# Plain columns in two halves of 336, up to five row blocks ahead of their norm, and the latent pairs interleaved

## The chip, the core and the metric

The kernel runs on one core of one Trainium2 chip. A time is the device time of one launch in microseconds (us), from the first to the last thing the core does for it; "before" is the median of three runs. Separate from these runs, one execution was recorded by the profiler, and all views of the profile and the trace come from that one. The engines are TensorE (PE in the rows; its weight loads are PEld), VectorE (DVE), ScalarE (ACT), GpSimd (POOL) and SyncE (SP), which issues most DMAs.

## The reference

One residual block over 1024 rows of 1024 columns, all in float32. Cut to what matters here:

```python
h = rmsnorm(x, mix_norm_g)
qa, ka, va, q_lat, kv_lat, k_r, g_a, g_b = split(h @ w_in)
#  512 128 128    384     256   32  1024 1024 columns
qa, ka = rope(qa), rope(ka)
o_a = sliding_window_attention(qa, ka, va, sinks)     # 8 heads, 2 kv heads, window 128
qb  = rmsnorm(q_lat, q_norm_g) @ w_uq                 # nope and rope part
kvb = rmsnorm(kv_lat, kv_norm_g) @ w_ukv              # k_nope and v
o_b = latent_attention(qb, kvb, rope(k_r))            # 8 heads, causal
y = sigmoid(g_a) * (o_a @ w_o_swa) + sigmoid(g_b) * (o_b @ w_o_mla)
x = x + y @ w_out
x = x + (silu(h2 @ w_gate) * (h2 @ w_up)) @ w_down    # h2 = rmsnorm(x, ffn_norm_g)
return rmsnorm(x, final_norm_g)
```

The change touches the first two lines and the first steps of the attention: the product of the normalised `x` with `w_in`, up to the point where the gate columns begin.

## The kernel before

**Products in halves.** A float32 operand is cut in a high part (ACT's cast, L160) and a low part (source minus high part, DVE, L163); this pair of instructions is `split` (L158). A product is then three passes on PE, high by high, high by low and low by high (`mm3`, L165 to L171: the three passes are lines L169, L170 and L171). Weights that carry the norm's gain are split with it (`split_g`, L229).

**Two kinds of columns of `w_in`.** The *plain* columns are multiplied as they stand: 512 columns of `qa` (`kvq`, L508; eight k-tiles of 128 rows by 512 columns, PSUM tile `kvq`) and 160 columns that hold `va` and `k_r` (`vk`, L483, tile `vk`), each once for each of the eight row blocks of 128 rows. The *latent* columns and `ka` (768 columns) go through a scheme with seven products instead of eight (`Seven`, L659): a pair j of column groups needs seven runs q = 1, 6, 2, 7, 5, 4, 3, each a product of one 512 by 128 weight (possibly a sum of quarters of the weight matrix) with one 512 by 512 quarter of `h`, or with a sum of quarters. A run is 12 passes of 512 columns. Three pairs, A, B and C, make 21 runs; `lat_head` (L985) is their order, and "A6" below is the run with j = A and q = 6. The gate columns use the same scheme behind it (`gates`).

**What a run needs.** The weight sums come from `mix` (L699; for the latent pairs six half-width instructions on POOL), after ACT scaled the weights by the gain (`scale_lt`, L916); a run's weight is split by `prep` (L713), tile `wl`. The sums of quarters of `h` come from `set_of_h` (L629), called once for each of four column groups c: it reads `h` back from memory (tiles `hr`, `ht`), subtracts, and splits the three results into `t1`, `t2`, `t3`. The run q = 6 multiplies by `t2`, 7 by `t3`, 5 by `t1`, 4 by `t4`; runs 1, 2 and 3 use the quarters of `h` themselves (`hh`, `hl`). The fourth sum is made on POOL at the end of `set_of_h` and split later (`t4_of_h`, L650).

**Where the rows of `h` come from.** For each row block b: `square(b)` (L460) takes the sum of squares on ACT and the factor `rn` on POOL; `spread(b)` (L468) lays the factor over the partitions by one small product; `normalize(b)` (L472) multiplies on DVE, and `to_quad(b)` (L475) splits the block into the quarter tiles. Blocks 0 to 4 (`RAW = 5`) are first split without their norm, so that `kvq` can start at once; `rope_q` (L499) multiplies their result by `rn` later, with the rotary tables, on DVE. `vk` of a block needs the normalised block. `vk_out` (L491) copies `v` and the rope key from PSUM. Block 0 is multiplied in plain float32 while its weights are split. `h_out` (L480) stores the normalised block for `set_of_h`, and `q_out` (L503) stores the rotated `qa` (`q_d`), which the sliding-window part loads back as `qn` and transposes on PE (`qT`).

**What follows a run.** `lat_done` (L962) takes the finished sum out of PSUM: for q-latent columns it scales, splits and stores it (`hi_lo_out`, L933, tile `cs`, store to `ct_d`) and squares it (`square_of`, L920); for the columns of `ka` it applies the rotation (`k_rope`, L947: four instructions on DVE, then a split into `ks`, stored to `ks_d`). The stores are issued by SP at the next `flush` (L942). Once all of `ks_d` is stored, four loads bring it back as `khd` for the first scores.

**The order.** Up to L1121 the order on PE, SP, ACT, DVE and POOL is written by hand: instructions stand in each engine's queue in the order of the calls. The plain part is L532 to L609 and L994 to L1044, with the calls `kvq`, `vk`, `normalize`, `to_quad` and so on; the latent runs are L1046 to L1120, one `lat_run(n)` (L989) each: it issues a run and then prepares weights up to the n-th. Tiles come from two pools with a fixed number of slots (U with 21, V with 17); a new tile waits until the last reader of its slot is done. [...]

Of the kernel before, what the change touches and what calls it, by code (L numbers as in the profile page):

```python
# [8 lines left out]
F32 = mybir.dt.float32  # L9
# [8 lines left out]
P = 128  # L18
# [24 lines left out]
VK = P + ROPE_B  # L43
# [44 lines left out]
def hybrid_block_kernel(  # L88
# [5 lines left out]
    w_x1: bass.AP,  # L94
    w_vk: bass.AP,
# [37 lines left out]
    psum_phase("psa", 4)  # L133
# [266 lines left out]
    w0 = st.raw[0] = U("wr", F32, (P, 2, 512))  # L400
# [3 lines left out]
    nc.scalar.dma_start(w0[:, 0], w_x1[:, 0])  # L404
# [3 lines left out]
    nc.sync.dma_start(w0[:, 1], w_x1[:, 1])  # L408
# [3 lines left out]
    st.load_to(3)  # L412
    load_xt(1)
    load_xt(2)
# [14 lines left out]
    def rope_nat(ps, heads, hw, cos, sin, outs, r=None):  # L429
        n = heads * 2 * hw  # L430
        t = U("rp")
        t1 = t[:, 0:n].rearrange("p (h t d) -> p h t d", t=2, d=hw)
        t2 = t[:, -n:].rearrange("p (h t d) -> p h t d", t=2, d=hw)
        cb = cos.unsqueeze(1).unsqueeze(1).to_broadcast([P, heads, 2, hw])
        sb = sin.unsqueeze(1).unsqueeze(1).to_broadcast([P, heads, 2, hw])
        for t_, b_ in ((t1, cb), (t2, sb)):
            if r is None:
                nc.vector.tensor_tensor(t_, ps, b_, op=ALU.mult)
            else:
                m_, p_ = (v.rearrange("p h t d -> p (h t) d") for v in (t_, ps))  # L440
                w_ = (cos if t_ is t1 else sin).unsqueeze(1).to_broadcast([P, heads * 2, hw])
                nc.vector.scalar_tensor_tensor(m_, p_, r, w_, op0=ALU.mult, op1=ALU.mult)
        for dst in outs:
            nc.vector.tensor_tensor(dst[:, :, 0], t1[:, :, 0], t2[:, :, 1], op=ALU.subtract)
            nc.vector.tensor_tensor(dst[:, :, 1], t1[:, :, 1], t2[:, :, 0], op=ALU.add)

    def halves(ap, hw):
        return ap.rearrange("p (h t d) -> p h t d", t=2, d=hw)

    def rope_of(ps, heads, b, r=None):  # L450
        qn = U("qn")
        rope_nat(halves(ps, 32), heads, 32, rope_a[:, 0, b], rope_a[:, 1, b], [halves(qn[:, 0:64 * heads], 32)], r)
        return qn

    wx1 = [halves_of((P, 2, 512), True) for _ in range(4)]
    kvq_ps, qns, sums, vk_ps = {}, {}, {}, {}
# [26 lines left out]
    def vk(b, mid=None):  # L483
        ps = vk_ps[b] = P1("vk", (P, VK))
        pairs = [(hT(k, blk(b)), tuple(w[:, k % 6] for w in wvk[k // 6])) for k in range(NK)]
        mm3(ps, pairs[:4], last=False)
        if mid is not None:
            mid()
        mm3(ps, pairs[4:], first=False)

    def vk_out(b):  # L491
        ps = vk_ps.pop(b)
        v_hi, v_lo = vv[b // 4][:, b % 4, :, 0:HD], vv[b // 4][:, b % 4, :, HD:P]
        v_ps = ps[:, 0:P].rearrange("p (g d) -> p g d", g=NG)
        nc.scalar.copy(v_hi, v_ps)
        nc.vector.tensor_tensor(v_lo, v_ps, v_hi.bitcast(F32), op=ALU.subtract)
        nc.scalar.copy(kr[:, 0, b], ps[:, P:VK])

    def rope_q(b):  # L499
        ps = kvq_ps.pop(b)  # L500
        qns[b] = rope_of(ps, 8, b, rn[:, b:b + 1] if b < RAW else None)
# [43 lines left out]
    for j in range(4):  # L545
        for k in (2 * j, 2 * j + 1):
            nc.tensor.matmul(ps, h0[:, k], raws[j][:, k % 2], start=k == 0, stop=k == NK - 1)
# [1637 lines left out]
```

## Time and profile before

| | us |
|---|---|
| three runs | 1386.88, 1385.52, 1385.92 |
| median | 1385.92 |
| profiled execution, its own time | 1383.58 |
| its span, first to last instruction | 1381.7 |
| PE busy in the span | 1322.0 |
| DVE, ACT, POOL busy | 931.2, 642.1, 586.7 |

The page lists busy time by engine, a bar of 40 slices of some 34.5 us each with the granted PE clock below it, and groups of instructions with the mean time of one and the idle time ahead of them. In rows of the trace the first number is the start in us from the span's start, the second the duration; x12 at a row's end means that several instructions alike stand in one row; a bracket at the end gives the idle time ahead of the instruction and what ended it. Rows name tiles without their numbers: `wl` is a split weight, `fa` and `fb` are the two kinds of PSUM tiles of the scheme with seven products.

### The profile page before, as it was taken

What the parts mean: (1) busy time and instruction counts of PE and PEld (TensorE: products, weight loads), DVE (VectorE), ACT (ScalarE), POOL (GpSimd) and SP (SyncE); (2) the same over time, 40 slices, a digit from 0 to 9 for tenths busy, and PEclk for the clock granted to TensorE, in tenths of its full rate; (3) what the DMA queues carried; (4) which work ended last, traced back from release to release, by engine and by line L of the source; (5) the groups of instructions that cost most, each with busy time, mean ns of one, the idle gap of its engine ahead of it and who ended that gap; (6) DMA issues with size and microseconds to landing.
All of it is one profiled execution on the core that took longest, in us unless ns stands there. A gap on an engine that the chain in (4) does not pass through costs nothing.

```text
span 1381.7 us, 18730 instructions
## 1 busy us (share of the span) xinstructions
PE 1322.0 (96%) x6376; PEld 1100.3 (80%) x6376; DVE 931.2 (67%) x1463; ACT 642.1 (46%) x1271; POOL 586.7 (42%) x627
## 2 busy tenths in 40 slices
PE   9964789999999999999999999999999999999997
PEld 6953578788878888988888888888888888888886
DVE  6754758778765877788787946656566565664763
ACT  6443246677534766774536422323223323644352
POOL 3063136556412554631232246778755552022421
PEclk9987889999999999999999999999999999999999
DMA  9721534553476847689742124555644324997504
GB/s 359 290 82 65 137 104 157 184 190 142 163 263 233 217 116 213 153 265 326 190 164 107 60 109 175 189 189 210 227 160 172 131 102 175 364 390 265 168 3 150
DMA packets 93456, 254.22 MB, mean 184 GB/s; under 512 B 10416, under 2 KB 16176, under 8 KB 91312
## 3 DMA queue, kind: packets, MB, share of 16 engines
q1 hardware_dynamic: 88496, 242.26, 50.2%
q0 software_dynamic: 3424, 8.39, 3.4%
q10 hardware_dynamic: 1440, 2.36, 0.5%
q8 instruction: 51, 0.84, 0.2%
q14 instruction: 45, 0.37, 0.1%
HBM read 166.60 MB, written 82.18 MB: 180 GB/s over the span
## 4 chain that ended last, share of the span: by engine, by line
PE 62%; issue 1%; POOL 1%; DVE 1%; ACT 0%; POOLq 0%; DVEq 0%
PE fa L171 6%; PE fa L169 6%; PE fa L170 6%; PE fd L170 5%; PE fd L171 5%; PE fd L169 5%; PE fb L170 4%; PE fb L171 4%; PE fb L169 4%; PE xo L171 2%; PE xo L170 2%; PE xo L169 2%; PE pTb L1348 1%; PE oB L171 1%; PE oB L170 1%
## 5 line engine op out<-in xcount | busy, mean ns | idle before, releaser
L163 DVE TENSOR_TENSOR wl<-wr,wl 128x512 fp32r<-128x512 f32 x165 | 156.0, 967 | 87.1 <-ACT wl L160 86.6
L163 DVE TENSOR_TENSOR lrv<-lr,lrv 128x1024 fp32r<-128x1024 f32 x77 | 105.5, 1402 | 47.8 <-ACT lrv L160 40.9
L160 ACT CAST lrv<-lr 128x1024 fp32r<-128x1024 f32 x77 | 80.1, 1052 | 87.2 <-PE fd L171 54.9
L169 PE MATMUL fd<-lrv 128*128 128x512 f32 x308 | 119.8, 389 | 0.0
L170 PE MATMUL fd<-lrv 128*128 128x512 f32 x308 | 119.8, 389 | 0.0
L171 PE MATMUL fd<-lrv 128*128 128x512 f32 x308 | 119.8, 389 | 0.0
L174 POOL TENSOR_TENSOR wr<-wr,sm 128x256 f32<-128x256 f32 (+1 forms) x44 | 50.7, 1165 | 137.9 <-DVE wl L163 122.4
L160 ACT CAST wl<-wr 128x512 fp32r<-128x512 f32 x165 | 95.6, 619 | 9.0 <-DVE t3l L174 2.8
L163 DVE TENSOR_TENSOR wl<-sm,wl 128x512 fp32r<-128x512 f32 x66 | 55.4, 860 | 42.7 <-ACT wl L160 41.3
L1333 POOL TENSOR_TENSOR denb<-denb,neg_one 128x1 f32<-128x1 f32 x64 | 41.5, 649 | 89.6 <-ACT p L1332 85.1
L169 PE MATMUL fa<-hh,wl 128*128 128x512 f32 x132 | 56.6, 429 | 21.6 <-ACT pu L761 18.2
L169 PEld LDWEIGHTS fd<-lrv 128*128 128x128 f32 x308 | 57.8, 188 | 12.1
L170 PEld LDWEIGHTS fd<-lrv 128*128 128x128 f32 x308 | 57.8, 188 | 12.0
L171 PEld LDWEIGHTS fd<-lrv 128*128 128x128 f32 x308 | 57.8, 188 | 12.0
L169 PE MATMUL fb<-t3h,wl 128*128 128x512 f32 x132 | 53.5, 405 | 11.5 <-ACT t4h L160 11.5
L1332 ACT ACTIVATE p<-scb,nmb 128x384 f32<-128x384 f32 (+3 forms) x64 | 47.7, 746 | 32.8 <-DVE nmb L1331 24.3
L1331 DVE CUSTOM_DVE_ANT_0 scb<-scb,mask,rlat 128x384 f32<-128x384 f32 (+3 forms) x64 | 52.1, 819 | 13.4 <-PE scb L1323 13.4
L171 PE MATMUL fa<-hh,wl 128*128 128x512 f32 x132 | 55.2, 418 | 0.2 <-DVE wl L163 0.2
L163 DVE TENSOR_TENSOR ptl<-pTb,pth 128x512 fp32r<-128x512 f32 (+2 forms) x96 | 49.9, 549 | 7.4 <-ACT pth L160 7.1
L170 PE MATMUL fa<-hl,wl 128*128 128x512 f32 x132 | 54.9, 416 | 0.0
L1706 ACT ACTIVATE act<-sm 128x512 f32<-128x512 f32 x11 | 7.0, 633 | 101.7 <-DVE sm L177 101.7
L170 PE MATMUL fb<-t3l,wl 128*128 128x512 f32 x132 | 53.1, 402 | 0.0
(371 smaller groups left out, 4163.8 us busy)
## 6 DMA issues: line engine op xcount, KB each, us to landing
lr<-la_d SPq DMA_DIRECT2D x77, 256.0 KB, 5.3
wr<-in_w_gate_dram SPq DMA_DIRECT2D x22, 512.0 KB, 4.2
wr<-in_w_up_dram SPq DMA_DIRECT2D x22, 512.0 KB, 4.9
la_d<-sd SPq DMA_DIRECT2D x22, 512.0 KB, 5.2
wd<-in_w_down_dram SPq DMA_DIRECT2D x22, 512.0 KB, 6.9
rb_d<-wd SPq DMA_DIRECT2D x22, 512.0 KB, 2.6
lr<-rb_d SPq DMA_DIRECT2D x44, 256.0 KB, 5.3
lr<-in_w_down_dram SPq DMA_DIRECT2D x33, 256.0 KB, 5.2
```

The costliest lines, as they stand in the source:

```text
L160: i = nc.scalar.copy(hi, src)
L163: (eng or nc.vector).tensor_tensor(lo, src, hi.bitcast(F32), op=ALU.subtract)
L169: nc.tensor.matmul(ps, ah, bh, start=first and i == 0, stop=False, skip_group_check=go_on)
L170: nc.tensor.matmul(ps, ah, bl, start=False, stop=False, skip_group_check=go_on)
L171: nc.tensor.matmul(ps, al, bh, start=False, stop=last and i == n - 1, skip_group_check=go_on)
L174: eng.tensor_tensor(out, a, b, op=ALU.subtract)
L1331: nc.vector.tensor_tensor_reduce(s_, s_, m_, rlat[:, n:n + 1], -NEG, op0=ALU.add, op1=ALU.min, accum_out=nm)
L1332: nc.scalar.activation(p_, s_, AF.Exp, scale=-1.0, bias=nm, accum_out=den)
L1333: nc.gpsimd.tensor_tensor(den, den, neg_one[:, 0:1], op=ALU.pow)
L1348: nc.tensor.transpose(pp[:, i], p[:, blk(k0 + i)], ident)
L1706: nc.scalar.activation(dst, src, AF.Silu)
```

## The change

**Plain columns.** `kvq` and `vk` give way to `nat(b, g)`: the plain columns are put together in two halves g of 336 columns (256 of `qa`, 64 of `va`, 16 of `k_r`), and both halves of a block are written to one PSUM tile `n` of two banks. The weights are loaded and split in units of three k-tiles. Blocks 0 to 4 are now multiplied without their norm in all their plain columns, and `row_out(b)` scales the copies of `v` and `k_r` and the rows of the rotary table by `rn` on ACT; the two rotary products on DVE then take the scaled table. Block 0 is in plain float32 in both halves (`nat0`).

**Rows and norms.** `norm_of(b)` is `normalize` and `to_quad` together. It stands up to five blocks behind the block's products, and blocks are normalised in the order 1, 5, 6, 2, 7, 0, 3, 4. The loads and squares follow that order.

**Sums of rows.** In `set_of_h` the subtraction that stood on POOL in two halves is one instruction on DVE, and the splits come in the order t2, t3, t1.

**Latent runs.** `lat_head` takes the first products of all three pairs ahead (A1, B1, C1, A2, B2, C2) and puts C's other runs between those of A and B. From the sixth run on a loop issues all of them and prepares two weights ahead of the run that it issues, that is, one ahead of the next. In this loop the loads of `qn` (`sw_q`) come ahead of the last `ks_d` stores and the `khd` loads, the load of `lg` and the store of the rope key come later, `gates.mix(0)` and the rotation of the rope key (`rope_kr`) go from DVE to POOL, and all gate scalings are on ACT.

```diff
-    for j in range(4):
-        plain(("x1", j), w_x1[:, 2 * j:2 * j + 2], (P, 2, 512), True, 2 * j)
-    plain(("vk", 0), w_vk[:, 0:6], (P, 6, VK), True, 0)
-    plain(("vk", 1), w_vk[:, 6:8], (P, 2, VK), False, 6)
+    for g in range(NG):
+        for u in range(3):
+            plain(("n", g, u), w_n[g, :, 3 * u:min(3 * u + 3, NK)], (P, min(3, NK - 3 * u), NW), True, 3 * u)
...
+    def scaled(b, dst, src):
+        if b < RAW:
+            nc.scalar.activation(dst, src, AF.Copy, scale=rn[:, b:b + 1])
+        else:
+            nc.scalar.copy(dst, src)
+    def row_out(b):
...
+        scaled(b, kr[:, 0, b].rearrange("p (g d) -> p g d", g=NG), ps[:, :, 320:NW])
+        scaled(b, v_hi, v_ps)
+        if b < RAW:
+            nc.scalar.activation(rope_a[:, :, b], rope_a[:, :, b], AF.Copy, scale=r)
...
+            nc.vector.tensor_tensor(t_, p_, w_, op=ALU.mult)
+        if b < RAW:
+            nc.vector.scalar_tensor_tensor(v_lo, v_ps, r, v_hi.bitcast(F32), op0=ALU.mult, op1=ALU.subtract)
...
+        sub(dst[:, :, 0], t1[:, :, 0], t2[:, :, 1], nc.vector)
+        add(dst[:, :, 1], t1[:, :, 1], t2[:, :, 0], nc.vector)
...
+    def nat(b, g, mid=None):
+        if g == 0:
+            n_ps[b] = PX("n", (P, 2, 512))
+        ps = n_ps[b][:, g, 0:NW]
...
+    nat(4, 0, lambda: spread(6))
+    h_out(5)
+    row_out(3)
+    nat(4, 1, lambda: spread(0))
+    norm_of(6)
+    q_out(3)
+    square(7)
+    norm_of(2)
+    square(4)
+    nat(5, 0, lambda: spread(7))
...
         sub(r[:, 0], t[:, 0], r[:, 0], nc.vector)
-        for k in range(0, 4, 2):
-            k = slice(k, k + 2)
-            sub(t[:, 0, k], t[:, 1, k], t[:, 0, k], nc.gpsimd)
-        between()
+        sub(t[:, 0], t[:, 1], t[:, 0], nc.vector)
         sub(t[:, 1], t[:, 1], r[:, 0], nc.vector)
-        for i, src in ((1, r[:, 0]), (3, t[:, 0]), (2, t[:, 1])):
+        for i, src in ((2, t[:, 1]), (3, t[:, 0]), (1, r[:, 0])):
             split_h(f"t{i}", c, src)
...
-        if j == 0:
-            nc.vector.tensor_scalar(t[:, k], t[:, k], g, None, op0=ALU.mult)
-        else:
-            nc.scalar.activation(t[:, k], t[:, k], AF.Copy, scale=g)
+        nc.scalar.activation(t[:, k], t[:, k], AF.Copy, scale=g)
...
-    lat_head = [(A, 1), (B, 1), (A, 2), (B, 2), (C, 1), (C, 2), (A, 6), (B, 6), (A, 7), (B, 7), (A, 5), (B, 5), (A, 4),
-                (B, 4), (A, 3), (B, 3)] + [(C, q) for q in (6, 7, 5, 4, 3)]
+    lat_head = [(A, 1), (B, 1), (C, 1), (A, 2), (B, 2), (C, 2), (A, 6), (B, 6), (A, 7), (B, 7), (A, 5), (C, 6), (B, 5),
+                (C, 7), (A, 4), (B, 4), (C, 5), (A, 3), (B, 3), (C, 4), (C, 3)]
...
+    for n in range(6, 21):
+        flush()
+        if n < 10:
+            t4_of_h(n - 6)
+        lat.prep_to(n + 2)
+        if n == 7:
+            lat.mix(C)
...
+        if n == 12:
+            sw_q(0)
+        if n == 14:
+            sw_q(1)
...
+        if n == 15:
+            k_load()
...
+        if n == 17:
+            gates.scale_part(0, 1)
+            gates.prep_to(1)
+            sw_qT(0)
+        if n == 18:
+            gates.mix(0)
+            gates.load_part(1, 0)
+        if n == 19:
+            gates.prep_to(2)
+        lat.run()
     flush()
     sw_scores(0)
+    gates.prep_to(3)
+    rope_kr()
```

**`set_of_h` on POOL and DVE.** Before, on POOL, between the two `mix` calls of A and B: the subtraction in two halves (`ht`) and the two halves of the fourth sum (`h`), for c = 2 and c = 3; `sm` and `wr` belong to `mix`.

```order
L174 TENSOR_TENSOR sm_891<-sm_891,wr_661 128x256
L174 TENSOR_TENSOR wr_661<-wr_661 128x2x128
L174 TENSOR_TENSOR ht_755<-ht_755 128x256 x2
L174 TENSOR_TENSOR h_133_931<-hr_754,ht_755 128x256 x2
L174 TENSOR_TENSOR ht_789<-ht_789 128x256 x2
L174 TENSOR_TENSOR h_133_931<-hr_788,ht_789 128x256 x2
L177 TENSOR_TENSOR sm_1011<-wr_707,wr_758 128x256
```

Now on POOL at the same place, for c = 1 and c = 2:

```order
L173 TENSOR_TENSOR sm_860<-sm_860,wr_728 128x256
L173 TENSOR_TENSOR wr_728<-wr_728 128x2x128
L173 TENSOR_TENSOR h_118_890<-hr_807,ht_808 128x256 x2
L173 TENSOR_TENSOR h_128_943<-hr_814,ht_815 128x256 x2
L176 TENSOR_TENSOR sm_959<-wr_811,wr_871 128x256
L173 TENSOR_TENSOR sm_959<-sm_959,wr_811 128x256
```

Before, on DVE, at c = 3 (the tiles with `hr_788` and `ht_789`), with the low parts of the weights of A2 and B2 ahead and of C1 behind:

```order
L163 TENSOR_TENSOR wl_954<-wr_705,wl_954 128x512
L163 TENSOR_TENSOR wl_972<-wr_758,wl_972 128x512
L174 TENSOR_TENSOR hr_788<-ht_789,hr_788 128x512
L174 TENSOR_TENSOR ht_789<-ht_789,hr_788 128x512
L163 TENSOR_TENSOR t1l_871<-hr_788,t1h_870 128x4x128
L163 TENSOR_TENSOR t3l_869<-ht_789,t3h_868 128x4x128
L163 TENSOR_TENSOR t2l_867<-ht_789,t2h_866 128x4x128
L163 TENSOR_TENSOR wl_1008<-wr_929,wl_1008 128x512
```

Now on DVE at c = 2 (tiles `hr_814`, `ht_815`), with the low part of the weight of C1 ahead and those of A2 and B2 behind:

```order
L162 TENSOR_TENSOR wl_925<-wr_911,wl_925 128x512
L173 TENSOR_TENSOR hr_814<-ht_815,hr_814 128x512
L173 TENSOR_TENSOR ht_815<-ht_815 128x512
L173 TENSOR_TENSOR ht_815<-ht_815,hr_814 128x512
L162 TENSOR_TENSOR t2l_885<-ht_815,t2h_884 128x4x128
L162 TENSOR_TENSOR t3l_887<-ht_815,t3h_886 128x4x128
L162 TENSOR_TENSOR t1l_889<-hr_814,t1h_888 128x4x128
L162 TENSOR_TENSOR wl_966<-wr_775,wl_966 128x512
L162 TENSOR_TENSOR wl_984<-wr_871,wl_984 128x512
```

The middle subtraction of a set has moved from POOL's queue into DVE's, between the other two, and t2's low part is now the first of the three.

**The loads of `qn` on SP.** SP's queue from the second half of the latent runs on; `wr` from `in_w_gt_dram` are the gates' first weights, `ct_d`, `ks_d` and `kr_d` are stores. Before:

```order
L944 DMA ct_d<-cs_1258 256x1x512
L777 DMA wr_1266<-in_w_gt_dram 128x1024
L944 DMA ks_d<-ks_1287 64x1x512 x4
L1094 DMA khd_1297<-ks_d 64x2048 x2
L1094 DMA khd_1300<-ks_d 64x2048 x2
L944 DMA ct_d<-cs_1317 256x1x512
L810 DMA qn_1327<-q_d 128x256
L810 DMA qn_1329<-q_d 128x256
```

and now:

```order
L791 DMA qn_1230<-q_d 128x256
L925 DMA ct_d<-cs_1246 256x1x512
L761 DMA wr_1254<-in_w_gt_dram 128x1024
L761 DMA wr_1256<-in_w_gt_dram 128x1024
L1061 DMA band<-c_band_dram 128x256
L1062 DMA nsink<-in_sinks_dram 128x8
L791 DMA qn_1276<-q_d 128x256
L925 DMA ks_d<-ks_1297 64x1x512 x4
L1040 DMA khd_1307<-ks_d 64x2048 x2
L1040 DMA khd_1310<-ks_d 64x2048 x2
L925 DMA ct_d<-cs_1327 256x1x512
```

The first load of `qn` stood behind the last `ks_d` stores and the four `khd` loads; both `qn` loads for the first scores now stand ahead of those.

**Weights and `k_rope` on ACT.** ACT's queue about the first `k_rope` (the cast into `ks`); each `wl` is the high part of one run's weight. Before, the casts ahead of `ks` are A5, B5 and A4 with the four casts of t4 between, and behind `ks` come B4, then A3:

```order
L160 CAST wl_1162<-sm_891 128x512
L160 CAST t4h_1144<-h_126_872 128x4x128
L160 CAST wl_1187<-sm_1011 128x512
L160 CAST t4h_1144<-h_133_931 128x4x128
L160 CAST wl_1205<-wr_705 128x512
L160 CAST t4h_1144<-h_133_931 128x4x128
L160 CAST ks_1230<-kc_1224 128x512
L160 CAST wl_1233<-wr_758 128x512
L938 ACTIVATE cs_1258<-sm_1011,latg 128x512
L926 ACTIVATE sq_1068<-sm_1011 128x512
L160 CAST wl_1262<-wr_705 128x512
L160 CAST ks_1287<-kc_1281 128x512
```

and now, the casts ahead of `ks` are B7, A5 and C6 and behind it come B5, C7, then A4 and B4:

```order
L159 CAST t4h_1090<-h_128_943 128x4x128
L159 CAST wl_1140<-wr_811 128x512
L159 CAST t4h_1090<-h_128_943 128x4x128
L159 CAST wl_1160<-sm_860 128x512
L159 CAST wl_1176<-sm_1115 128x512
L159 CAST ks_1199<-kc_1193 128x512
L159 CAST wl_1206<-sm_959 128x512
L159 CAST wl_1227<-wr_911 128x512
L919 ACTIVATE cs_1246<-sm_959,latg 128x512
L907 ACTIVATE sq_1065<-sm_959 128x512
L159 CAST wl_1251<-wr_775 128x512
```

The first `k_rope` follows the run A5 in both orders. Behind A5's cast there stood the casts of two more runs (B5, A4) ahead of `ks`, and now that of one (C6).

More of the change, by code (lines that the diff above doesn't have):

```diff
@@ L535, in hybrid_block_kernel @@
         nc.tensor.matmul(P1("warm"), warm[:, 0:P], warm, start=True, stop=True)
-    raws = [st.raw.pop(j) for j in range(4)]
-    st.n_conv = 4
+    raws = [st.raw.pop(j) for j in range(6)]
+    st.n_conv = 6
     h0 = U("h0", F32, (P, NK, P))
```

376 lines of the change are left out of this document (147 added, 229 removed).

## The prediction

> **What bounds the kernel now.** I read the page first, then PE's waits, then the busy time by stretch, then the timeline of the stretch that stands out.
>
> ```profile
> PE 1322.0 (96%) x6376; PEld 1100.3 (80%) x6376; DVE 931.2 (67%) x1463; ACT 642.1 (46%) x1271; POOL 586.7 (42%) x627
> ...
> PEclk9987889999999999999999999999999999999999
> ```
>
> TensorE (PE) is busy for 96% of the span, so only time in which it idles or runs at a lower granted clock can be won. The clock row dips only in its second to sixth digit, that is between about 70 and 205 us. PE's waits between 70 and 192 us (summed us, times, longest):
>
> ```profile
> PE fa L169 <- ACT pu L761: 18.2, 3, 8.8
> PE qT L818 <- DMA qn<-q_d: 11.6, 1, 11.6
> PE fb L169 <- ACT t4h L160: 11.5, 1, 11.5
> PE fa L169 <- ACT wl L160: 2.1, 1, 2.1
> ```
>
> Six waits, 43.4 us. Busy time by stretch (PE, PEld, DVE, ACT, POOL, then granted clock, DMA):
>
> ```profile
> 0.00:75.00 75.00, 72.36 (x400) 58.57 (x401) 55.07 (x100) 41.87 (x89) 17.27 (x36) 1.00 0.86 321
> 75.00:191.00 116.00, 72.52 (x266) 56.26 (x264) 63.96 (x102) 39.74 (x83) 39.80 (x44) 0.78 0.30 87
> 191.00:1381.70 1190.70, 1177.08 (x5715) 985.52 (x5713) 812.17 (x1262) 560.53 (x1099) 529.65 (x549) 1.00 0.55 185
> ```
>
> Three stages. Up to 75 us (the plain columns) PE is full. From 75 to 191 us (the latent products) it idles 43.5 of 116 us at clock 0.78, and none of ACT, DVE and POOL is full either: that is a stage of chains between engines. After 191 us PE is busy for 99%, and the order listings agree there on every engine, so what the front gains arrives at the end. Four places of PE in time:
>
> ```profile
> 74.95 0.28 PE L171 MATMUL vk<-wh,hl 128*128 128x160 f32 x1
> 75.06 0.43 PE L169 MATMUL fa<-hh,wl 128*128 128x512 f32 x1
> ...
> 116.13 0.63 PE L169 MATMUL fb<-t2h,wl 128*128 128x512 f32 x1
> ...
> 133.66 0.77 PE L169 MATMUL fb<-t3h,wl 128*128 128x512 f32 x1 [11.53 <-ACT t4h L160]
> ...
> 191.00 0.39 PE L169 MATMUL fa<-hh,wl 128*128 128x512 f32 x1
> ...
> 193.72 0.28 PE L818 MATMUL qT<-ident_r,qn 128*128 128x128 f32 x2
> ```
>
> The first latent run (A1) begins at 75.06, its seventh (A6) at 116.13, the ninth (A7) at 133.66, the first gate run at 191.00; that run's twelve passes end at 193.72, so a run is 2.72 us and a 512-wide pass 0.227. Twenty-one runs are 57.1 us of work in 115.9. The releaser named "pu" had long been done. What was late there is seen one engine further, in the waits of DVE and ACT from 75 to 120 us:
>
> ```profile
> DVE ht L174 <- POOL ht L174: 9.3, 3, 4.2
> ACT t3h L160 <- POOL ht L174: 7.3, 3, 3.6
> ```
>
> One of the subtractions of `set_of_h` stands on POOL, behind the six halves of `mix`, and both other queues wait for it with the next weight splits behind them.
>
> **The change, step by step.** I walk DVE's, ACT's and PE's new orders with measured durations.
>
> *Products.* The widths nearest to 336 are 320 and 384:
>
> ```profile
> 580.97 0.31 PE L1321 MATMUL scb<-kT,qT 96*128 96x320 f32 x1
> 581.12 0.31 PE L1322 MATMUL scb<-kT,qT 96*128 96x320 f32 x1
> ...
> 570.67 0.34 PE L1322 MATMUL scb<-kT,qT 96*128 96x384 f32 x1
> 570.85 0.34 PE L1323 MATMUL scb<-kT,qT 96*128 96x384 f32 x1
> ...
> 7.93 5.59 PE L547 MATMUL kvq<-wr,h 128*128 128x512 f32 x12 [0.44 <-DMA wr<-in_w_x_dram]
> 13.20 2.26 PE L515 MATMUL kvq<-wv,hh 128*128 128x512 f32 x8
> ```
>
> Start to start 0.15 and 0.18; a quarter of the way gives 0.152. A block was 24 passes of 0.227 and 24 of 0.11, 8.1 us; it becomes 48 x 0.152 = 7.3. Block 0 is now raw fp32 in both halves: 32 records, 0.44 each at 512 columns (7.93 to 13.20 for twelve), 0.29 by proportion (bounds 0.29 and 0.44, 9.3 to 14.1 us; I take the lower, since the widths above scale). Begun at 5.5: 9.3 for block 0, 7.3 for block 1, 1.7 estimated for weight splits that come just late, so 23.8; six blocks 43.8 and eight spreads at about 0.25 put PE's end at 69.6.
>
> But A1 needs what DVE prepares behind the blocks:
>
> ```profile
> 51.19 1.22 DVE L473 TENSOR_TENSOR xt<-xt,rb 128x1024 f32<-128x1024 f32 x1
> 53.09 1.29 DVE L163 TENSOR_TENSOR hl<-xt,hh 128x512 fp32r<-128x512 f32 x2 [0.69 <-ACT hh L160]
> ...
> 67.53 0.29 DVE L496 TENSOR_TENSOR vv<-vk,vv 128x128 fp32r<-128x128 f32 x1 [2.10 <-ACT vv L495]
> ...
> 69.79 0.68 DVE L174 TENSOR_TENSOR hr<-ht,hr 128x512 f32<-128x512 f32 x1
> ```
>
> One `norm_of` takes 3.2 us (51.19 to 54.38), the DVE part of one row block 2.3 (67.53 to 69.79: the same four kinds of operation that `row_out` issues). From about 34.0, when block 2 is out, DVE has five rows (11.5) and seven norms (22.4) to do, and stands some 2.9 behind ACT, whose copies queue behind a square or a scaling: 70.8, and 71.4 with A1's low part. A1 thus finishes near 74.0 and not at 77.8: the better part of the narrower products is hidden behind DVE. The move of squares and raw splits costs nothing beyond this; DMA is as full as before in this stage.
>
> *The four sets, A1 to A6.*
>
> ```profile
> L163 DVE TENSOR_TENSOR t3l<-ht,t3h 128x512 fp32r<-128x512 f32 x3 | 3.6, 1214 | 0.0
> L163 DVE TENSOR_TENSOR t1l<-hr,t1h 128x512 fp32r<-128x512 f32 x3 | 2.1, 685 | 0.0
> L160 ACT CAST wl<-wr 128x512 fp32r<-128x512 f32 x15 | 9.2, 616 | 5.9 <-issue 1.9 <-POOL sq L177 1.4 <-DVE wl L163 1.3
> ...
> 86.80 1.70 ACT L918 ACTIVATE wr<-wr,gT 128x256 f32<-128x256 f32 x4
> ```
>
> With POOL quiet a DVE subtraction is 0.69, with POOL at work up to 1.21. A set becomes three subtractions, one cast of 0.62 and three low parts: 4.8 quiet, 6.9 beside a `mix`. Two sets stand beside `mix`, two beside the two POOL halves of t4, so 23.6 in all. Row block 7 adds 2.3, five low parts of splits 4.4, waits for ACT's scalings (1.70 for four, before B1, A2 and C2) 3.9. 71.4 + 34.2 = 105.6 for A6's split; A6 ends near 108.8, against 118.9 before (116.13 + 2.72): **10 us won**. The six runs are 16.3 us of work in this stretch, so PE still waits, in four places of 1.5 to 6 us. Of the splits' slots in this stretch only C1's waits for the run just ahead (B1), and that run is done by then.
>
> *A7.* B6 follows directly. A7's split stands on ACT behind the square of C2, which waits for A6's end by its slot, and two casts of t4; on DVE behind two low parts beside POOL. I count 5.6 us from A6's end to the split's end, 114.4; A7 ends near 118. Before, it began at 133.66 and ended about 138, slow at first: **another 10 us**. The 11.5 us wait there hung on a slot:
>
> ```profile
> 126.74 0.60 ACT L930 ACTIVATE sqt<-fa 128x512 f32<-128x512 f32 x1 [3.89 <-DMA ct_d<-cs]
> ```
>
> the square waited for the store of `cs`, and POOL and A7's split stood behind it. In the new order the stores of B2 and C2 are issued before A6 ends or just after, and the split's slot waits for the first of them.
>
> *A7's end to the gates.* Twelve runs, 32.6 us. Before they took 53 us, 11.6 of them the wait for `qn`, which now is loaded ahead of the four `khd` loads. What is late next: splits are prepared one run less ahead, and `k_rope` stands between.
>
> ```profile
> 143.84 0.69 DVE L177 TENSOR_TENSOR sm<-fa,sm 128x512 f32<-128x512 f32 x1 [0.76 <-PE fa L171]
> ...
> 148.12 0.69 DVE L163 TENSOR_TENSOR ks<-kc,ks 128x512 fp32r<-128x512 f32 x1 [0.73 <-ACT ks L160]
> ```
>
> From A5's end this chain is 5.0 us; then comes B5's low part, 0.7. C6 covers 2.72 of it, so B5 waits about 2.8; C5 the same after A4; C4 about 2.9 behind the gates' scalings (3.4 on ACT); small waits 1. Each wait also costs half speed afterwards:
>
> ```profile
> 96.40 0.79 PE L169 MATMUL fa<-hh,wl 128*128 128x512 f32 x1 [2.26 <-ACT pu L761]
> ...
> 97.42 0.63 PE L171 MATMUL fa<-hh,wl 128*128 128x512 f32 x1
> 97.85 0.63 PE L169 MATMUL fa<-hh,wl 128*128 128x512 f32 x1
> ```
>
> After 2.26 us of idling the passes are 0.43 apart. I take 1.4 us for each of the three. So 32.6 + 8.5 + 1 + 4.2, less what overlaps, 43.5: the last latent run ends near 161.8, the first scores (eight short passes, 0.85) at 162.7. This replaces the 191.00 of before: **28.3 us in all**.
>
> [...]
>
> *What moves to POOL at the end.* `rope_kr` and the gates' first `mix`:
>
> ```profile
> L177 POOL TENSOR_TENSOR sm<-wr,wr 128x256 f32<-128x256 f32 x6 | 6.1, 1023 | 2.1 <-DVE wl L163 2.1
> ...
> 163.29 2.42 SPq L1094 DMA_DIRECT2D khd<-ks_d  x4
> 176.45 0.50 PE L818 MATMUL qT<-ident_r,qn 128*128 128x128 f32 x2 [11.60 <-DMA qn<-q_d]
> ```
>
> At about 1.0 each, `mix` is 6 us and `rope_kr` 3 to 4; behind them on POOL stand the three last sums of squares and the first softmax's norm, which the first transposes of the loop wait for some 18 us after the gates begin. I cost it at nothing; without that cover it is up to 10. The `khd` loads were issued at 163.29 and done by 176.45 at the latest (`qn` came behind them); issued near 148.5 now, they land near 161, a little ahead of the scores.
>
> **Sum.** The profiled execution took 1383.58 us (span 1381.7 and 1.9 around it), 2.3 below the median 1385.92. Less 28.3 that is 1355.3 on its own time, 1358 on the median's. About 0.2% (2.8 us) is what a measurement of this kernel can tell from no change.
>
> **Rivals.**
> - *The chains vanish.* If DVE and ACT pack better than I walk them, PE runs 21 x 2.72 from 69.6 to 126.7; then `khd` decides: after A4 it needs the 5.0 chain, the stores (about 5) and some 12 to land, 22 against six runs of 16.3, plus 0.85 for the scores: 133, a gain of 58, 1328. For it: no engine is full in the stage. Against it: the orders are in line, and each set is a round trip. Between this and the forecast I keep 1326 to 1345.
> - *The sets don't get shorter.* The subtraction on DVE meets `mix` on POOL (1.21 for 0.69), and A6 comes no earlier than 116; the later gains stay. Or POOL's ten microseconds show at the first softmax. Either gives back about 10: 1368.
> - *It doesn't do what it says.* A slot or a store in the new order holds a split as `cs` did for 11.5 us, twice, and the gain is gone: 1386.
> - *Slower: every split behind the run before it.* The latent splits are prepared one ahead. If each slot came free only with the preceding run, a run would cost 2.72 + 0.62 + 0.69 and 1.6 of half speed, 5.6; 21 of them 118, the two `k_rope` chains 7 more, from 69.6 to 195 instead of 190: 1391. The point of decision: more than 3.0 us of waiting a run on the mean (before: 2.8). Against it: the listing shows such a wait for few splits.
>
> **How the numbers follow.** Forecast (1346 to 1367) 0.52; chains vanish 0.12; 10 given back (1367 to 1380) 0.22; nothing left 0.05; slower 0.09. The range leaves out the slower cases and the fast end: 1341 to 1380. With the bounds: block 0 in fp32 adds at most 4.8, the half speed takes 4.2 off, POOL adds 10. Faster 0.86, same 0.05, slower 0.09.
>
> **What would show it.** In the changed kernel's trace: A1 between 69 and 73; A6 near 104 to 108; no wait of a transpose for `qn`; waits of 2 to 3 us at B5 and C5; the first gate run near 163; after it the same length as before, 1190. Wrong would be a wait of more than 6 us anywhere in the latent runs, an A1 later than 75, or a tail longer than before.

## The result and the profile after

| | before | changed |
|---|---|---|
| median of four runs, us | 1386.4 | 1371.73 |
| lowest and highest | 1385.52, 1388.06 | 1370.65, 1373.15 |
| profiled execution, its own time | 1383.58 | 1373.15 |
| its span | 1381.7 | 1371.4 |

The four runs of before are the three named above and one more; the profiled execution of the changed kernel is one of its four. The changed kernel is faster by 1.07% (ratio 0.9893, 95% interval 0.9876 to 0.9911), 14.7 us at the medians. The two profiled executions differ by 10.4 us only: that of before lies 2.8 below the median of its four runs, that of the changed kernel 1.4 above. The page of the changed kernel, busy time of TensorE and the granted clock in 40 slices:

```profile
PE 1324.3 (97%) x6368; PEld 1105.7 (81%) x6368; DVE 931.3 (68%) x1452; ACT 645.3 (47%) x1284; POOL 585.8 (43%) x629
...
PEclk9989979999999999999999999999999999999999
```

The clock now dips in the third and the sixth slice only; the fourth and fifth are back at 9. PE's waits in the first 200 us of the changed kernel (summed us, times, longest):

```profile
PE fa L168 <- ACT wl L159: 13.9, 5, 4.9
PE sc L821 <- DVE qs L805: 4.9, 1, 4.9
...
```

The waits of 7 to 12 us of before (for `pu`, `t4h` and `qn`) are gone. The longest are 4.9 us, one of them (the second scores, `sc`) at a place where PE did not wait before. Busy time of PE by stretch, cut at PE's landmarks (us, busy, granted clock, DMA share). Before, from the first latent pass to the first gate run, from there to the first transposes of the probabilities (`pT`), and the rest:

```profile
75.06:191.00 115.94, 72.46 (x265) 0.78 0.30 87
191.00:208.95 17.95, 17.77 (x91) 0.90 0.31 103
208.95:1381.70 1172.75, 1159.32 (x5625) 1.00 0.55 186
```

The changed kernel, cut at the same three places:

```profile
70.36:165.95 95.59, 71.47 (x264) 0.91 0.50 160
165.95:193.79 27.84, 22.98 (x93) 0.69 0.27 94
193.79:1371.40 1177.61, 1161.43 (x5625) 1.00 0.55 185
```

The first gate run is 25.05 us earlier (165.95 for 191.00). The first transposes are 15.2 us earlier (193.79 for 208.95): between these two landmarks the changed kernel takes 27.8 us where before took 18.0, at clock 0.69 instead of 0.90. Places of PE in the timeline of the changed kernel:

```profile
70.36 0.39 PE L168 MATMUL fa<-hh,wl 128*128 128x512 f32 x1
...
74.14 0.50 PE L170 MATMUL fa<-hh,wl 128*128 128x512 f32 x1 [3.15 <-DVE wl L162]
...
85.88 0.79 PE L168 MATMUL fa<-hh,wl 128*128 128x512 f32 x1 [4.87 <-ACT wl L159]
...
107.18 0.51 PE L168 MATMUL fb<-t2h,wl 128*128 128x512 f32 x1 [0.24 <-ACT wl L159]
...
115.24 0.47 PE L168 MATMUL fb<-t3h,wl 128*128 128x512 f32 x1 [1.27 <-ACT wl L159]
...
165.95 0.45 PE L168 MATMUL fa<-hh,wl 128*128 128x512 f32 x1
...
176.77 0.58 PE L821 MATMUL sc<-khd,qs 128*128 128x256 f32 x1 [4.86 <-DVE qs L805]
...
178.74 6.82 PE L1095 MATMUL st<-neg_one,sq 128*128 128x1 f32 x32
185.42 0.77 PE L168 MATMUL fa<-hh,wl 128*128 128x512 f32 x1
...
193.79 0.46 PE L859 MATMUL pT<-ident_r,per 128*128 128x128 f32 x4
```

Before, from the first scores on:

```profile
184.60 0.22 PE L840 MATMUL sc<-khd,qs 128*128 128x128 f32 x1
...
196.97 0.39 PE L840 MATMUL sc<-khd,qs 128*128 128x256 f32 x1
...
198.31 3.63 PE L1132 MATMUL st<-neg_one,sq 128*128 128x1 f32 x32
```

A1 begins at 70.36 (before 75.06), A6 at 107.18 (116.13), A7 at 115.24 (133.66). Behind the first gate run (165.95) PE waits 4.86 us at the second scores; the 32 one-column products `st` behind them take 6.82 us, where before took 3.63, and the next gate run starts its passes 0.43 apart.

### The profile page after: what moved, and what is told of

Read it like the earlier page. It is cut to its first block, busy times and chain, and to the rows that moved or that the text cites. A ratio compares the mean times of both kernels' runs of the same rounds, so it can differ in the third digit from the quotient of the medians.

```text
span 1371.4 us, 18705 instructions
## 1 busy us (share of the span) xinstructions
PE 1324.3 (97%) x6368; PEld 1105.7 (81%) x6368; DVE 931.3 (68%) x1452; ACT 645.3 (47%) x1284; POOL 585.8 (43%) x629
## 4 chain that ended last, share of the span: by engine, by line
PE 61%; DVE 2%; issue 2%; POOL 1%; ACT 0%; POOLq 0%; DVEq 0%; ACTq 0%
PE fa L170 5%; PE fa L169 5%; PE fa L168 5%; PE fd L169 5%; PE fd L168 5%; PE fd L170 5%; PE fb L169 4%; PE fb L170 4%; PE fb L168 4%; PE xo L170 2%; PE xo L168 2%; PE xo L169 2%; PE pTb L1311 1%; PE oB L170 1%; PE oB L168 1%
## 5 line engine op out<-in xcount | busy, mean ns | idle before, releaser
L162 DVE TENSOR_TENSOR wl<-wr,wl 128x512 fp32r<-128x512 f32 x165 | 159.1, 986 | 82.6 <-ACT wl L159 82.1
L176 POOL TENSOR_TENSOR sm<-wr,wr 128x256 f32<-128x256 f32 (+1 forms) x42 | 46.6, 1109 | 32.6 <-ACT wr L899 20.0
L168 PE MATMUL fa<-t1h,wl 128*128 128x512 f32 x132 | 52.4, 397 | 4.5 <-ACT wl L159 4.5
```

Source lines behind the costliest of these rows:

```text
L162: (eng or nc.vector).tensor_tensor(lo, src, hi.bitcast(F32), op=ALU.subtract)
L168: nc.tensor.matmul(ps, ah, bh, start=first and i == 0, stop=False, skip_group_check=go_on)
L176: eng.tensor_tensor(out, a, b, op=ALU.add)
```

## The experiments

Twelve kernels in three questions. Times are medians of four or more runs, each with the ratio to the kernel before on the same chip. The last column is the start of the first `pT` in the profiled execution, which is the sharper measure of the front: from there to the end the 14 profiled executions took between 1172.7 and 1177.6 us, whatever the edit, and that spread is in every total. The first latent pass, for one and the same plain part, moved by up to 2 us between executions; so differences of `pT` under about 1.5 us are not read.

| kernel | median, us | ratio (95% interval) | first `pT`, us |
|---|---|---|---|
| before | 1386.4 | 1 | 208.95 |
| changed | 1371.73 | 0.9893 (0.9876 to 0.9911) | 193.79 |
| scores one run earlier | 1368.03 | 0.9876 (0.9854 to 0.9898) | 189.93 |
| gate load later | 1371.98 | 0.9907 (0.9880 to 0.9935) | 193.59 |
| both of these | 1368.63 | 0.9885 (0.9857 to 0.9912) | 193.24 |
| POOL's work back on VectorE | 1370.72 | 0.9898 (0.9876 to 0.9921) | 194.11 |
| store ahead of `khd` | 1365.12 | 0.9862 (0.9830 to 0.9894) | 190.62 |
| store ahead, scores earlier | 1366.88 | 0.9857 (0.9831 to 0.9884) | 187.54 |
| plain part alone | 1382.89 | 0.9985 (0.9970 to 1.0000) | 205.66 |
| subtraction back on POOL | 1373.72 | 0.9911 (0.9892 to 0.9930) | 197.51 |
| old order of the runs | 1371.53 | 0.9896 (0.9881 to 0.9911) | 195.84 |
| A1's split ahead of row block 6 | 1370.09 | 0.9889 (0.9875 to 0.9904) | 194.06 |
| before, queries earlier | 1382.90 | 0.9984 (0.9972 to 0.9996) | 208.54 |
| before, queries earlier, gate work behind C6 | 1378.88 | 0.9963 (0.9951 to 0.9975) | 202.26 |

### Where ten microseconds went behind the first gate run

ACT's timeline in the changed kernel, ahead of the second scores:

```profile
166.66 1.71 ACT L767 ACTIVATE wr<-wr,gT 128x256 f32<-128x256 f32 x4 [2.77 <-DMA wr<-in_w_gt_dram]
...
168.80 0.71 ACT L919 ACTIVATE cs<-pu,latg 128x512 fp32r<-128x512 f32 x1
...
172.77 0.37 ACT L837 ACTIVATE pe<-sc,nm 128x128 f32<-128x128 f32 x1 [2.74 <-DVE nm L829]
...
175.51 0.38 ACT L803 CAST qs<-qT 64x256 fp32r<-64x256 f32 x1
```

and SP's issues:

```profile
149.87 2.42 SPq L1040 DMA_DIRECT2D khd<-ks_d  x4
152.33 0.60 SPq L925 DMA_DIRECT2D ct_d<-cs  x1
...
162.70 0.33 SPq L761 DMA_DIRECT2D wr<-in_w_gt_dram  x1
```

Before, ACT had the exponentials of the first scores ahead of these four scalings, and ahead of the first gate run (191.00):

```profile
187.71 0.37 ACT L856 ACTIVATE pe<-sc,nm 128x128 f32<-128x128 f32 x1 [1.49 <-DVE nm L848]
...
193.64 1.71 ACT L786 ACTIVATE wr<-wr,gT 128x256 f32<-128x256 f32 x4
```

The second scores need the second queries (`qs`). Their cast on ACT (175.51) stands behind the exponentials of the first scores (from 172.77). These waited for VectorE's row maxima, which stood behind a `cs` on VectorE, which waited for ACT's `cs` (168.80), which stood behind four scalings of the second gate pair's weight (`wr`), which waited until 166.66 for their load. That load was issued at 162.70 only. As I read it, its slot of the pool was held by an earlier `cs` until that was stored, and the store was issued (152.33) behind the 2 MB of the `khd` loads. Two theories: the chain lacks cover (before the change two latent runs stood between the first scores and the first gate run, now none), or the late weight does it. POOL's moved work is the third.

```diff
+        if n == 20:
+            sw_scores(0)
         lat.run()
     flush()
-    sw_scores(0)
```

> The changed kernel with the first scores of the sliding window one latent run earlier (ahead of C3, the last one). Theory 'lost cover': the chain from the first scores through their row maxima, exponentials and the split of the second queries is longer than the two gate runs behind it, so the wait of 4.9 us at the second scores falls by about one run (2.7) to 1.5 to 2.5, the half-speed stretch behind it gets shorter, and the time falls by 4 to 9 us against the changed kernel (1371.7), to 1363 to 1368. Rival 'late weight': ACT's scalings of the second gate weight still hold the exponentials until that load lands near 166.7, so the wait stays above 4 us and the time within 2 us. Rival 'POOL': no change either, since the sums and the rotation of the rope key on POOL stay where they are.

The wait at the second scores fell from 4.86 to 1.72 us, `pT` came 3.9 us earlier (some 0.5 of it lay ahead of A6 already), the time is 1368.0. Lost cover is a cause; the half-speed stretch did not go (passes behind `st` are still 0.43 apart, 182.9 to 186.4 us).

```diff
             gates.mix(0)
-            gates.load_part(1, 0)
...
     sw_scores(0)
+    gates.load_part(1, 0)
```

> The changed kernel with the load of the second gate pair's first weight issued behind the first scores, as before the change; ACT's four scalings of it then stand behind the split of the second queries. Theory 'lost cover': the chain loses the 2.8 us of waiting and the 1.7 us of scaling only in part (VectorE's share of it stays), the wait falls from 4.9 to 2 to 3.5, the time by 1 to 5 us, to 1367 to 1371. Rival 'late weight': the wait is under 1 us, the half-speed stretch is gone, and the time falls by 8 to 10 us, to 1362 to 1364.

> Both moves together. Either theory: no wait of over 1 us at the second scores, no half speed between 174 and 191 us, and the time falls by 8 to 10 us against the changed kernel, to 1362 to 1364. If the wait is gone and the time is not 8 us lower, the half-speed stretch has another cause (the 32 one-column products behind the second scores).

Both expectations failed. The wait at the second scores did fall (1.77 and 1.30 us), but a new one of 3.16 and 2.60 us stood ahead of it at C3, and `pT` stayed at 193.6 and 193.2. ACT in the first of the two kernels, and PE:

```profile
162.28 0.72 ACT L919 ACTIVATE cs<-pu,latg 128x512 fp32r<-128x512 f32 x1 [5.37 <-DMA ct_d<-cs]
```

```profile
164.09 0.79 PE L168 MATMUL fa<-hh,wl 128*128 128x512 f32 x1 [3.16 <-ACT wl L159]
...
178.35 0.39 PE L821 MATMUL sc<-khd,qs 128*128 128x256 f32 x1 [1.77 <-DVE qs L805]
```

With the load gone from this place, the next `cs` got its slot, and waited 5.37 us for the same store; the split of C3 stands behind it on ACT. So what is late is neither the weight nor its load: it is the slot behind the store behind `khd`. Whoever takes the slot waits. (That the medians of the two kernels differ by 3.3 us at the same `pT` is the spread of the rest.)

```diff
-        if n == 15:
+        if n == 16:
             k_load()
+        if n == 15:
             nc.vector.tensor_scalar(nsink, nsink, -1.0, None, op0=ALU.mult)
```

> The changed kernel with the khd loads issued one run later, behind the store of cs that stood behind them. Theory 'slot behind the store': the slot of that cs is what the second gate weight's load waits for; the load is issued near 157 in place of 162.7 and has landed before ACT comes to the scalings, so ACT does not wait 2.8 us, the wait at the second scores falls from 4.9 to 1.5 to 3, and the first transposes of the probabilities stand 2 to 6 us earlier than 193.8; the time falls by as much if the khd loads still land before the first scores (165). Rival 'khd late': the first scores wait for khd by 1 to 3 us and nothing is won.

SP's issues now:

```profile
148.16 0.55 SPq L925 DMA_DIRECT2D ct_d<-cs  x1
...
149.46 2.58 SPq L1040 DMA_DIRECT2D khd<-ks_d  x4
152.15 0.53 SPq L761 DMA_DIRECT2D wr<-in_w_gt_dram  x1
```

The store stands ahead of `khd`, the load of the weight follows at 152.15 instead of 162.70, and ACT waits 0.18 us for it. The wait at the second scores is 3.29 us, a little over the expected range; `pT` comes 3.2 us earlier (the first scores stand 0.8 us earlier already, 164.30 for 165.11), and the first scores do not wait for `khd`.

> Both: the khd loads one run later and the first scores one run earlier. Theory: the wait at the second scores is under 1 us, the first transposes of the probabilities stand at 186 to 189 (the changed kernel alone 193.8, with the scores one run earlier 189.9), and the time is 1364 to 1367. Rival 'khd late': the first scores, now at 163.5, wait for khd by more than 1 us and the transposes are at 190 or later.

Both edits together: `pT` at 187.54, 6.25 us earlier than in the changed kernel, near the sum of the two (3.9 and 3.2), with a wait of 1.29 us left (expected under 1). Medians of 1365.1 and 1366.9 lie too close to rank the two kernels. Either is faster than before; against the changed kernel it is `pT` that shows the gain, for the intervals of the ratios overlap with that of the changed kernel.

> The changed kernel with the gates' first sums and the rotation of the rope key back on VectorE. Theory 'lost cover': POOL was not late at the first softmax (it waited 0.43 us for ACT there), so nothing is won; VectorE gets some 6 us more work between 156 and 172 us, and the time is the same to 4 us longer, 1371 to 1376. Rival 'POOL': the first norm comes 2 to 5 us earlier and the time falls by 3 to 10 us.

`gates.mix(0, nc.vector)` and `rope_kr` on VectorE as before: PE at the second scores:

```profile
178.88 0.39 PE L821 MATMUL sc<-khd,qs 128*128 128x256 f32 x1 [4.07 <-DVE qs L805]
```

The wait is 4.07 us, and `pT` is 0.3 later: POOL's work was not the loss, and moving it there was not a gain in this place.

### Which part of the change made the gain

The plain part as changed, with `set_of_h`, `lat_head`, `scale_gate` and the latent calls of before:

> The plain part of the change (two halves of 336, norms up to five blocks behind, other order of loads and squares) with the latent part of before (order of the runs, one subtraction of each set on POOL, loads of the queries behind the khd loads). Theory 'latent part': TensorE is done with the plain columns some 5 us earlier, but the sets begin no earlier than before since VectorE is late, so the waits of the latent runs grow by what was won: the first gate run within 4 us of before (191.0), the time 1380 to 1388. Rival 'plain part': most of the gain is there, 1370 to 1376.

The time is 2.3 us lower than before, inside the expectation, though the interval reaches 1.0000; the first gate run begins at 187.7, 3.3 us earlier. The wait ahead of A7 is there as before:

```profile
131.61 0.77 PE L168 MATMUL fb<-t3h,wl 128*128 128x512 f32 x1 [11.53 <-ACT t4h L159]
```

```diff
-        sub(t[:, 0], t[:, 1], t[:, 0], nc.vector)
+        for k in range(0, 4, 2):
+            k = slice(k, k + 2)
+            sub(t[:, 0, k], t[:, 1, k], t[:, 0, k], nc.gpsimd)
```

> The changed kernel with the one subtraction of each set back on POOL in two halves, as before the change, all else as changed. Theory: it stands behind mix on POOL again and VectorE and ACT wait for it with the next weights behind them; A6 starts at 111 to 116 in place of 107.2, and the time is 3 to 8 us longer, 1375 to 1380. Rival 'hidden': the runs ahead of A6 wait for the loads and scalings of C's and B's weights anyway, so A6 moves by less than 1.5 us and the time by less than 2.

```profile
110.04 0.51 PE L168 MATMUL fb<-t2h,wl 128*128 128x512 f32 x1 [0.96 <-ACT wl L159]
```

A6 comes 2.9 us later (110.04 for 107.18), `pT` 3.7. That is less than the theory said and more than the rival: the move is worth about a third of what A6 won. The median is 2.0 us longer, which the intervals do not tell from nothing.

The changed kernel with the list `lat_head` of before:

> The changed kernel with the order of the 21 latent runs of before (A1 B1 A2 B2 C1 C2, then A's and B's runs, C's last five at the end); the loop prepares one ahead as changed. Theory 'interleaving covers the rotation': B5 and B4 stand directly behind A5 and A4 and wait for the 5 us chain of k_rope with no run of C between: their waits grow from 2.1 to about 5, half speed follows, and the first transposes of the probabilities stand 4 to 9 us later than 193.8; the time is 1375 to 1381. Rival 'order is free': within 2 us, since the head A1 to C2 waits for the sets in any order.

```profile
108.90 0.79 PE L168 MATMUL fa<-hh,wl 128*128 128x512 f32 x1 [10.53 <-ACT pu L745]
```

The sixth run, C2 in both orders, waits 10.53 us and A6 begins at 114.19, 7.0 us later than with the new order. But `pT` is only 2.1 us later, the median the same: PE's wait at the second scores is 1.63 us here. What the new order wins by A6, it gives back behind the gates, so no gain of the order alone is shown in the time. The expected waits of 5 us at B5 and B4 did not come (0.2 and none); PE waited one run later, 2.12 us at A4 and 3.88 at A3. The theory fell.

```diff
-    row_out(6)
     nat(7, 1)
...
+    lat.prep_to(1)
+    row_out(6)
     q_out(6)
-    lat.prep_to(1)
```

> The changed kernel with the split of A1's weight ahead of the rotation and copies of row block 6 on ACT and VectorE. Theory 'sets decide': the 3.15 us wait inside A1 goes and A1 ends near 74.5 in place of 77.5, but C1 begins at 84 to 87 as now, since its split stands behind the first set and the scalings of C's weight; the first transposes of the probabilities stay within 1.5 us of 193.8. Rival 'A1 passes it on': C1 and all behind it come 2 to 3 us earlier, 190.5 to 192.

```profile
76.40 0.80 PE L168 MATMUL fa<-hh,wl 128*128 128x512 f32 x1 [4.02 <-ACT wl L159]
...
85.80 0.80 PE L168 MATMUL fa<-hh,wl 128*128 128x512 f32 x1 [3.92 <-ACT wl L159]
```

A1's passes run through, and B1 waits 4.02 us instead; C1 begins at 85.80, as in the changed kernel (85.88). ACT's timeline of the changed kernel says why:

```profile
83.47 1.71 ACT L899 ACTIVATE wr<-wr,gT 128x256 f32<-128x256 f32 x4 [2.36 <-DMA wr<-in_w_lt_dram]
```

C's weight lands at 83.47, and its scaling and split follow. The load decides C1, not the set ahead of it; in that the expectation's reason was wrong, though its numbers for C1 and `pT` held (A1 ended near 72.2, where 74.5 was expected).

### Whether the load of the queries was the lock

```diff
+    sw_q(0)
+    sw_q(1)
     flush()
     for g in range(NG):
         khd.append(V("khd", F32R, (P, 2, S)))
...
-    sw_q(0)
-    sw_q(1)
```

> The kernel before with one edit: the two loads of the first queries are issued ahead of the last ks_d stores and the khd loads. Theory: the wait of 11.6 us at the first query transpose goes; the first scores then come at 173 to 176 and wait for khd by 0 to 3 us; the first transposes of the probabilities stand 7 to 11 us earlier than 208.95, at 198 to 202, and the time is 1375 to 1379. Rival 'khd decides': the wait moves to the first scores nearly whole, and the gain is under 3 us.

```profile
176.60 0.77 PE L169 MATMUL fb<-t3h,wl 128*128 128x512 f32 x1 [9.88 <-DVE pu L177]
```

The transposes, now at 166.44, no longer wait, and the next run, C7, waits 9.88 us. Neither theory named that: the median is 1382.90, where the theory said 1375 to 1379, and the rival's gain of under 3 us came without its reason. VectorE in this kernel:

```profile
172.67 1.13 DVE L784 TENSOR_SCALAR wr<-wr,gT 128x256 f32<-128x256 f32 x4
173.83 0.69 DVE L177 TENSOR_TENSOR sm<-wr,wr 128x512 f32<-128x512 f32 x1
...
175.77 0.68 DVE L177 TENSOR_TENSOR pu<-fb,pu 128x512 f32<-128x512 f32 x1
```

C7 goes on adding to the PSUM tile `fb` of C6, so it must wait until VectorE has taken C6's sum out (`pu<-fb`, 175.77); that stood behind the gates' four scalings and three sums.

```diff
-    gates.prep_to(1)
     lat_run(19)
-    gates.mix(0, nc.vector)
     flush()
     lat_run(20)
+    gates.prep_to(1)
+    gates.mix(0, nc.vector)
```

> The kernel before with two edits: the queries loaded earlier, as in the run before, and the preparation of the first gate weight with the gates' first sums (four scalings, one split, four scalings, three sums on VectorE) behind C6 in place of ahead of it. Theory 'two locks': with the queries there, C7 waited 9.9 us for C6's sum to be taken out of PSUM, since that stood on VectorE behind this gate work; with the gate work behind it C7 begins at 169 to 172 (176.6 with the one edit), the first transposes of the probabilities stand at 201 to 205 (208.5 with the one edit), and the time is 4 to 7 us below the one edit's, 1376 to 1379. Rival 'a third lock': the khd loads or the split of the queries hold the first scores to 182 or later, and the transposes stay within 2 us of 208.5.

```profile
169.57 0.76 PE L169 MATMUL fb<-t3h,wl 128*128 128x512 f32 x1 [4.16 <-DVE pu L177]
```

C7 begins at 169.57, `pT` stands at 202.26, 6.3 us earlier than with the one edit, and the time is 4.0 us lower (on another chip; by the ratios to before, 0.9963 for 0.9984). There were two locks on one door; the row of the wait named the one that opened last.

## Why the prediction was right, and where it was not

**Direction and range** were right: forecast 1358, range 1341 to 1380, measured 1371.73. The gain was half of what was forecast (14.7 of 28.3), near the rival "10 given back" (1368), but by another way than that rival's two. So that the time fell inside the range is in part luck: its slow part was there for the sets and for POOL, and neither gave anything back. One reading was off by a digit: the clock row of before dips in its third to sixth digit, not from the second on; the times given with it are right.

**Products.** PE ended the plain columns at 70.36 (forecast 69.6), as worked out. **A1** was to finish near 74.0; it finished near 77.5, since its low part came late. VectorE ahead of it, in the changed kernel:

```profile
71.11 0.98 DVE L173 TENSOR_TENSOR qn<-rp 128x256 f32<-128x256 f32 x1
72.02 0.94 DVE L176 TENSOR_TENSOR qn<-rp 128x256 f32<-128x256 f32 x1
72.88 1.21 DVE L162 TENSOR_TENSOR wl<-wr,wl 128x512 fp32r<-128x512 f32 x1
```

The subtraction and the add of row block 6 took 0.98 and 0.94 us, where I had counted about 0.4 each, and the low part 1.21 where 0.69 is the quiet figure (before, between 141 and 159 us, with no operation on POOL): POOL's `mix` runs beside them, six operations from 71.08 to 76.2 us. After the wait of 3.15 us half speed followed (clock 0.50 from 75.4 to 78.8 us). So the plain part alone won little, as "the better part of the narrower products is hidden behind DVE" had said; the run with this part alone shows 2.3 us, at the edge of what its interval tells from none.

**Sets, A1 to A6.** Forecast: A6's split at 105.6; A6 began at 107.18, against 116.13. Four waits of over 1.5 us ahead of it (3.15, 4.87, 2.13, 2.40), as said. On VectorE the four sets took 5.3, 5.4, 7.1 and 5.3 us, 23.0 in all for the 23.6 of the walk (whose 6.9 for a set beside `mix` is less than six operations of 1.21 and a cast, 7.9). The size held and its composition did not: undoing the subtraction costs 2.9 us, undoing the new order 7.0 (more together than the 8.95 won, so the two overlap), and C1's start hangs on the load of C's weight, which the walk had left out. **A7** was to begin at 114.4 and began at 115.24. The square that had waited for the store of `cs` waits for no store now (0.89 us for VectorE instead); the stores are issued from 109.33 on, where the last of them had been issued at 123.66. That was the largest single term, 9.5 us between A6 and A7. With the latent part of before the 11.53 us are there; with the old order of the runs, or with the subtraction on POOL, they are not. That leaves the loop, which issues the stores earlier; no run undoes the loop alone.

**A7 to the gates.** Waits of about 2.8 at B5, 2.8 at C5 and 2.9 at C4 were forecast; 2.08, 2.41 and 2.30 (1.64 and 0.66) were measured. Half speed was charged three times, at an estimated 1.4 us each, and came once, at C5 (clock 0.50 from 147.0 to 150.4 us); behind the waits at B5 and C4 the clock stayed at 1.00. The first gate run was forecast at 162.7 and began at 165.95: 25.05 us won there, of 28.3. But the cause I gave for one term was too simple: "11.6 of them the wait for `qn`". In before the earlier load alone moves `pT` by 0.4 us, since the gate work on VectorE was a second lock. In the changed kernel that lock is gone as well: B5 stands between C6 and C7, and the run with the gate work back on VectorE is no slower.

**The step that failed** is "after 191 us ... the order listings agree there on every engine, so what the front gains arrives at the end", and with it "after it the same length as before, 1190". It was 1205.4 in the profiled execution: 9.9 us more between the first gate run and the first `pT`, and 4.9 more behind them, which is the spread between executions. Of the 9.9 us 4.86 are PE's wait at the second scores and 3.2 the `st` products at half speed behind it. So the prediction's own sign of being wrong, "a tail longer than before", came. PE's listing does agree from the first gate run on. Those of ACT and VectorE do not: the first scores, which the sum counts as "eight short passes, 0.85", had stood two latent runs ahead of the first gate run and now stand directly ahead, so their softmax has moved from ahead of that run to behind it (ACT's exponentials at 187.71 for 191.00, now at 172.77 for 165.95), and behind the four scalings. From the first scores to PE's being ready for the second there were 12.4 us before (184.60 to 196.97) and 6.8 now. The chain over VectorE and ACT and back took 8.4 to 12.4 us, from the first scores to the second, in the ten kernels where PE waited for it and no other wait lay between; the two of 8.4 and 8.5 (old order, gate load later) are those where none of ACT's four scalings stands in it. The runs gave back 3.9 us for the cover and 3.2 for the slot, 6.25 for both. I looked for this loss on POOL, where there was none: "behind them on POOL stand ... the first softmax's norm" was costed with its cover, and the same softmax on ACT and VectorE was not. Of the remaining 3.6 us 0.8 lie ahead of the first gate run (166.79 for 165.95) and 2.8 behind it, where a wait of 1.29 us is left and half speed lasts 6.8 us (before 3.4); they were not taken apart further.

## What to carry to other kernels

Where a change moves a step past others, measure for each chain that starts there how long it runs and how much work of the bounding engine still stands between its start and its first reader; equal order on the bounding engine behind the step says nothing of that. A wait's releaser is the last lock, not the only one (here 11.60 us at `qn` went and 9.88 came at C7): before costing its removal, ask when the next need of the same instruction, and of the one behind it, is met. A tile's slot inherits the lateness of its last reader, so a store should not be issued behind bulk loads when the slot is soon wanted; moving one user away hands the wait to the next (2.77 us for `wr`, then 5.37 for `cs`).

## What the runs showed of the clock

By the granted clock, the half-speed stretches in the first 200 us of the changed kernel begin at 75.4, 85.6, 92.4, 102.7, 147.0 and 174.3 us; the first five last 3.41 us each, the sixth 17.1. So I cut PE's time into windows of 3.41 us, one behind the other, that fall on these starts (length, busy us, granted clock, DMA):

```profile
112.92:116.33 3.41, 1.76 (x7) 1.00 0.40 154
143.61:147.02 3.41, 1.66 (x6) 1.00 0.16 41
147.02:150.43 3.41, 3.41 (x11) 0.50 0.59 138
181.13:184.54 3.41, 3.41 (x17) 0.50 0.02 5
```

The window with 1.76 us of work at full clock is followed by full clock (passes behind 116.33 are 0.23 apart), the one with 1.66 by half clock in the whole next window. Of the 2.41 us of idling at C5 (until 145.29) 1.7 lie in the second of these. The 2.08 us at B5 (until 130.84) fall on two windows with 2.21 and 2.46 us of work, and the 2.30 at C4 (the last until 158.91) on two with 2.03 and 2.49; the clock is 1.00 in these four and in the windows behind them. So 2.41 us of idling went with half clock here, 2.08 and 2.30 with full; what sets the clock was not shown.

The last row holds only the one-column products `st`: by the row PE is busy throughout, and the clock stays at one half (0.50), until 191.4 us. Before the change the same products, run at full clock, are followed by a half-speed window:

```profile
198.68:202.09 3.41, 3.41 (x31) 1.00 0.57 195
202.09:205.50 3.41, 3.41 (x10) 0.51 0.00 0
```

In the changed kernel the clock is 0.50 ahead of the 32 one-column products, beside them and behind them; before, it is 1.00 beside them and 0.51 behind. What in these products goes with the low clock was not shown, and whether spreading them out would save it was not tried.
